# Four buffers of split weights in the expert stage, and products with the low part issued behind both column halves

## The chip, the core and the metric

The kernel runs on one core of one Trainium2 chip. The metric is the device time of one execution in microseconds (us), the median of several runs. An engine is named as the profile names it: PE is TensorE's matmul, PEld its weight load, DVE VectorE, ACT ScalarE, POOL GpSimd, SP SyncE, which issues most of the DMAs.

## What is computed

One layer of a hybrid encoder on 1024 tokens of width 2048 in float32: attention over a window and long convolutions side by side, an output projection, and then a mixture of 16 experts in which each expert picks its 128 tokens. The change lies in the experts alone:

```python
gate, idx = lax.top_k(jnp.swapaxes(affinity, 1, 2), cap)          # 16 experts, 128 tokens each
xg = jax.vmap(lambda hb, ib: hb[ib])(h, idx)
a = jnp.einsum('becd,edf->becf', xg, w_gate)                      # 2048 -> 1024
up = jnp.einsum('becd,edf->becf', xg, w_up)                       # 2048 -> 1024
ye = jnp.einsum('becf,efd->becd', jax.nn.silu(a) * up, w_down)    # 1024 -> 2048
ye = ye * gate[..., None].astype(ye.dtype)
# ... and each row of ye is added to the row of its token
```

## The kernel before

To keep float32 accuracy with the faster reduced float type, each operand is split in two: a high part, the value rounded by a copy on ACT (line 60), and a low part, what is left, by a subtraction on DVE (line 61). A product is then three matmuls (`mm3`, line 70): high token by high weight, high token by low weight, low token by high weight. In the expert stage (`phase3`) the tokens are the stationary operand and the weights stream, 512 columns at a time.

The raw weights of an expert come as 24 tiles of 1 MB: eight of the gate and eight of the up matrix in turn, then eight of the down matrix. They lie in a ring of 19 buffers (`EW`), taken in order by `load_expert`; two of the first expert's tiles lie in `el0` and `el1`, which later hold the expert's intermediate result `y` and its transposed, split form `h3`. SP issues a load as soon as its buffer has been let go. A raw tile is two half tiles of 128 x 1024; each is split into a pair `wh3`, `wl3`, of which there are three, so a new split has to wait until the matmuls of the third half tile before it have ended.

`gate_up` runs six steps of gate and up, half tile after half tile, six matmuls each (two column halves `n` of 512, three products). The last four raw tiles, the tail, are kept and gone through by column half: first all four half tiles for `n` = 0, then for `n` = 1, each step with the gate's 512 columns and the up's beside one another in one pair of split buffers. So the first column half of the result is ready early: `act(0)` makes SiLU(gate) x up of it (ACT line 1130, DVE line 1131), and `turn(0)` transposes it on TensorE in the third step of `n` = 1. `down` does the same with the down matrix, `turn(1)` behind its second raw tile, and the transposes of the next expert's tokens (`xh`, `xl`, from the gather of line 1090) behind the fourth to the seventh. Then ACT copies four banks with the gate's factor into `y` (line 1176) and POOL adds its rows to the output. Six PSUM banks are taken in turn by the two functions.

The order on TensorE is the program's, by `manual_schedule`. The orders on ACT, DVE and SP are laid down at compile time by the framework, which may put an instruction ahead of another that stands before it in the program; on the chip each of these engines then goes through its queue strictly in that order.

Of the kernel before, what the change touches and what calls it, by code (L numbers as in the profile page):

```python
# [8 lines left out]
R = mybir.dt.float32r  # L9
# [8 lines left out]
P = 128  # L18
D = 2048
S = 1024  # L20
KD = D // P
# [4 lines left out]
FF = 1024  # L26
# [11 lines left out]
class Block:  # L38
# [885 lines left out]
                            self.lane.append((t, c, first[t], xs[t]))  # L924
                        yield

    EW, EA = 19, 3
    EX = 2
    NW = KD + FF // P

# [138 lines left out]
    def phase3(self, ctx):  # L1069
        tc, nc, a = self.tc, self.nc, self.a  # L1070
        self.topk()
        pa = ctx.enter_context(tc.tile_pool(name="pa", bufs=1, space=PSUM, reuse_waits="tile"))
        pt_ = ctx.enter_context(tc.tile_pool(name="pt3", bufs=2, space=PSUM, reuse_waits="tile"))

        ex = ctx.enter_context(tc.tile_pool(name="ex", bufs=1, reuse_waits="tile"))
        self.ring(ctx, "ewb", 2, side="right")
        self.ring(ctx, "ewc", 8)
        el = self.el = ctx.enter_context(tc.tile_pool(name="el", bufs=1, reuse_waits="tile"))
        self.ring(ctx, "ewd", 6)
        xh = ex.tile([P, KD, P], R, name="xh", bufs=1)  # L1080
        xl = ex.tile([P, KD, P], R, name="xl", bufs=1)

        def bank():
            return pa.tile([P, 512], F32, name="pa", bufs=6)

        def gather(e):
            if e == NE:
                return
            xg = ex.tile([P, D + 16], F32, name="xg", bufs=1)
            nc.gpsimd.indirect_dma_start(out=xg, out_offset=None, in_=self.xg[:, :],  # L1090
                                         in_offset=bass.IndirectOffsetOnAxis(ap=self.idx[:, e:e + 1], axis=0))
            return xg

        def load():
            ahead = self.EW + max(min(self.used, KD - self.EX) + self.EX, self.used)
            while self.loaded < min(ahead, NE * self.NW):
                self.load_expert()

        def raw():
            load()  # L1100
            self.used += 1
            return self.eraw.pop(0)

        def parts():
            return (el.tile([P, FF], R, name="wh3", bufs=3), el.tile([P, FF], R, name="wl3", bufs=3))

        def half(w, i):
            wh, wl = parts()
            self.split(wh, wl, w[:, i * FF:i * FF + FF])
            return wh, wl  # L1110

        def gate_up(e):


            xg = self.xg3
            rs = ex.tile([P, 16], F32, name="rs", bufs=1)
            nc.scalar.copy(rs[:, 0:1], xg[:, D:D + 1])
            ps = {}
            for n in range(2):
                for j in range(2):  # L1120
                    ps[j, n] = bank()
            y = el.tile([P, 2 * FF], F32, name="el0", bufs=1)
            h3 = el.tile([P, 2, FF // P, P], R, name="el1", bufs=1)

            def product(j, n, k, wh, wl):
                self.mm3(ps[j, n], xh[:, k], xl[:, k], wh, wl, k == 0, k == KD - 1)

            def act(n):
                s = y[:, n * 512:n * 512 + 512]
                nc.scalar.activation(s, ps[0, n], AF.Silu, scale=rs[:, 0:1])  # L1130
                nc.vector.scalar_tensor_tensor(s, ps[1, n], rs[:, 0:1], s, op0=ALU.mult, op1=ALU.mult)

            def turn(n):
                self.turned(pt_, h3[:, 0], h3[:, 1], y, n)

            for kk in range(KD // 2 - 2):
                if kk == 2:
                    self.xg3 = gather(e + 1)
                for j in range(2):
                    w = raw() if kk or e else None  # L1140
                    for i in range(2):
                        wh, wl = half(w, i) if w is not None else ready.pop(0)
                        for n in range(2):
                            sl = slice(n * 512, n * 512 + 512)
                            product(j, n, 2 * kk + i, wh[:, sl], wl[:, sl])

            w = [raw() for j in range(4)]
            for n in range(2):
                for i in range(4):
                    wh, wl = parts()  # L1150
                    for j in range(2):
                        sl = slice(j * 512, j * 512 + 512)
                        c = i % 2 * FF + n * 512
                        self.split(wh[:, sl], wl[:, sl], w[i // 2 * 2 + j][:, c:c + 512])
                        if n == j == 1 and i == 2:
                            turn(0)
                        product(j, n, KD - 4 + i, wh[:, sl], wl[:, sl])
                act(n)
            return h3, y, lambda: turn(1)

        def down(e, h):
            h3, y, rest = h
            ps = [bank() for n in range(4)]
            for k in range(FF // P):
                w = raw()
                for c in range(2):
                    wh, wl = half(w, c)
                    for n in range(2):
                        sl = slice(n * 512, n * 512 + 512)
                        self.mm3(ps[2 * c + n], h3[:, 0, k], h3[:, 1, k], wh[:, sl], wl[:, sl], k == 0, k == FF // P - 1)  # L1170
                if k == 1:
                    rest()
                elif 3 <= k < 7 and self.xg3 is not None:
                    self.turned(pt_, xh, xl, self.xg3, k - 3, 2)
            for n in range(4):
                nc.scalar.activation(y[:, n * 512:n * 512 + 512], ps[n], AF.Copy, scale=self.gate[:, e:e + 1])  # L1176
            nc.gpsimd.indirect_dma_start(out=a["out"],
                                         out_offset=bass.IndirectOffsetOnAxis(ap=self.idx[:, e:e + 1], axis=0),
                                         in_=y, in_offset=None, compute_op=ALU.add)

        self.xg3 = gather(0)
        ready = []
        for j in range(2):
            w = raw()
            ready += [half(w, i) for i in range(2 - j)]
        ready.append(None)
        with tc.manual_schedule(engines={mybir.EngineType.PE}):
            for kg in range(4):
                self.turned(pt_, xh, xl, self.xg3, kg, 2)
            ready[3] = half(w, 1)  # L1190
            for e in range(NE):
                down(e, gate_up(e))
# [96 lines left out]
```

## Time and profile before

| | us |
|---|---|
| median of 3 runs (3375.63 to 3378.23) | 3376.8 |
| the profiled execution | 3381.3 |
| its span, first to last instruction | 3379.5 |
| TensorE busy in it | 3239.7 (96%) |
| VectorE busy | 2342.4 (69%) |
| ScalarE busy | 1848.0 (55%) |

The expert stage begins at about 2206 us, when the choice of tokens is done, and takes the rest of the span, about a third. TensorE's busy time counts a matmul from its start to its modelled end, and successive ones overlap; how densely they follow is read from their starts. The granted clock of TensorE is given as a share of full speed.

### The profile page before, as it was taken

The page shows a single profiled execution, that of the slowest core. Times are in us where ns is not written, and L with a number is a line of the kernel's source. Part 1 is how long each engine was busy: PE and PEld are TensorE (multiplying, and loading weights), DVE is VectorE, ACT ScalarE, POOL GpSimd, SP SyncE. Part 2 cuts the span into 40 slices and gives each one's busy share as a digit, 9 for nine tenths or more (in the row PEclk, how much of TensorE's full clock was granted, in tenths as well). Part 3 has the DMA queues.
Part 4 walks back from the last instruction along what each step waited for, and adds up shares of the span by engine and source line. Part 5 has one row for each costly group of instructions (what it writes and reads, how often), then busy time and mean ns, then how long its engine had stood idle before and what let it go on. Part 6 is the DMA issues. An engine that isn't in the chain of part 4 may idle for free.

```text
span 3379.5 us, 47125 instructions
## 1 busy us (share of the span) xinstructions
PE 3239.7 (96%) x17232; PEld 2794.5 (83%) x17232; DVE 2342.4 (69%) x3626; ACT 1848.0 (55%) x2956; POOL 87.9 (3%) x200
## 2 busy tenths in 40 slices
PE   8999999999999999999999999579999999999998
PEld 7899999987888888889977878467888877777776
DVE  5677766664666767667653333578889988888887
ACT  5455655443333433334453332258888877777776
POOL 0000000000000000000000000000000000000000
PEclk9999999999999999999999999789999999999999
DMA  7654555456566565555567554569999999999993
GB/s 244 198 166 163 167 173 194 159 157 221 181 197 194 191 196 184 194 193 167 168 213 240 188 200 138 217 262 376 377 393 387 389 382 370 375 384 365 384 379 107
DMA packets 286568, 830.67 MB, mean 246 GB/s; under 512 B 26341, under 2 KB 105360, under 8 KB 229761
## 3 DMA queue, kind: packets, MB, share of 16 engines
q1 hardware_dynamic: 280544, 791.12, 64.4%
q0 software_dynamic: 5648, 36.49, 4.1%
q8 instruction: 135, 2.21, 0.3%
q14 instruction: 97, 0.79, 0.1%
q10 hardware_dynamic: 144, 0.07, 0.0%
HBM read 751.71 MB, written 75.60 MB: 245 GB/s over the span
## 4 chain that ended last, share of the span: by engine, by line
PE 83%; DMA 6%; DVE 4%; ACT 4%; issue 2%; SPq 0%; POOLq 0%; POOL 0%; ACTq 0%; DVEq 0%
PE pj L68 29%; PE pa L68 27%; PE o L68 7%; PE c L68 5%; PE f L68 4%; PE a L68 3%; PE ct L79 2%; ACT wh L60 2%; DVE wl L61 2%; DMA w<-in_w_out_dram 2%; PE tp L1200 1%; PE a L79 1%; PE ft L79 1%; ACT el L1176 1%; DMA hl<-lo_d 1%
## 5 line engine op out<-in xcount | busy, mean ns | idle before, releaser
L60 ACT CAST wh<-w 128x1024 fp32r<-128x1024 f32 (+3 forms) x1368 | 1072.3, 795 | 778.8 <-PE pj L68 383.5
L61 DVE TENSOR_TENSOR wl<-w,wh 128x1024 fp32r<-128x1024 f32 (+3 forms) x1368 | 1219.6, 905 | 361.7 <-ACT wh L60 340.6
L68 PE MATMUL pa<-wl,xh 128*128 128x512 f32 x1024 | 409.0, 399 | 14.0 <-DVE wl L61 14.0
L68 PE MATMUL pa<-wh,xh 128*128 128x512 f32 x1024 | 407.8, 398 | 9.4 <-ACT wh L60 9.4
L68 PE MATMUL pa<-wh,xl 128*128 128x512 f32 x1024 | 404.8, 395 | 0.0
L68 PE MATMUL pa<-wh,el 128*128 128x512 f32 x1024 | 340.6, 399 | 0.0
L68 PE MATMUL o<-wh,m 128*128 128x512 f32 x1008 | 332.1, 403 | 0.7 <-ACT wh L60 0.7
L68 PE MATMUL pj<-wh,hh 128*128 128x384 f32 x896 | 315.9, 353 | 2.9 <-ACT wh L60 2.9
L68 PE MATMUL pj<-hh,wh 128*128 128x512 f32 x768 | 314.7, 410 | 0.0
L68 PE MATMUL pj<-hl,wh 128*128 128x512 f32 x768 | 304.8, 397 | 6.4 <-DMA hl<-lo_d 6.4
L68 PE MATMUL pj<-wl,hh 128*128 128x384 f32 x896 | 305.1, 341 | 0.0
L68 PE MATMUL pj<-wh,hl 128*128 128x384 f32 x896 | 304.3, 340 | 0.0
L68 PE MATMUL pj<-hh,wl 128*128 128x512 f32 x768 | 302.9, 395 | 0.0
L68 PEld LDWEIGHTS pa<-wl,xh 128*128 128x128 f32 x1024 | 193.5, 189 | 70.6 <-DVE wl L61 27.1
L68 PEld LDWEIGHTS pa<-wh,xh 128*128 128x128 f32 x1024 | 193.3, 189 | 58.5 <-ACT wh L60 13.4
L68 PEld LDWEIGHTS pa<-wh,xl 128*128 128x128 f32 x1024 | 193.4, 189 | 43.5
L68 PEld LDWEIGHTS pa<-wh,el 128*128 128x128 f32 x1024 | 193.1, 189 | 39.5
L68 PEld LDWEIGHTS o<-wh,m 128*128 128x128 f32 x1008 | 191.0, 191 | 39.0 <-ACT wh L60 1.8
L68 PE MATMUL pa<-wl,el 128*128 128x512 f32 x512 | 201.3, 393 | 0.0
L68 PE MATMUL o<-wl,m 128*128 128x512 f32 x504 | 198.9, 395 | 0.3 <-DVE wl L61 0.3
L68 PEld LDWEIGHTS pj<-wh,hh 128*128 128x128 f32 x896 | 169.7, 189 | 8.8 <-ACT wh L60 3.2
L68 PEld LDWEIGHTS pj<-hh,wl 128*128 128x128 f32 x768 | 144.5, 188 | 34.7
(304 smaller groups left out, 5301.5 us busy)
## 6 DMA issues: line engine op xcount, KB each, us to landing
hl<-lo_d SPq DMA_DIRECT2D x608, 256.0 KB, 3.0
w<-in_w_down_dram SPq DMA_DIRECT2D x128, 1024.0 KB, 11.2
w<-in_w_up_dram SPq DMA_DIRECT2D x127, 1024.0 KB, 8.1
w<-in_w_gate_dram SPq DMA_DIRECT2D x127, 1024.0 KB, 9.6
w<-in_w_at_dram SPq DMA_DIRECT2D x120, 384.0 KB, 3.5
w<-in_w_out_dram SPq DMA_DIRECT2D x64, 512.0 KB, 3.9
w<-in_w_hy_dram SPq DMA_DIRECT2D x96, 256.0 KB, 3.4
Hd<-H SPq DMA_DIRECT2D x32, 513.0 KB, 4.2
```

The lines of the kernel that those rows point to most:

```text
L60: nc.scalar.copy(hi, src)
L61: nc.vector.tensor_tensor(lo, src, hi.bitcast(F32), op=ALU.subtract)
L68: self.nc.tensor.matmul(out, w, x, start=start, stop=stop)
L79: self.nc.tensor.transpose(pt[:, i * P:(i + 1) * P], b, self.ident)
L1176: nc.scalar.activation(y[:, n * 512:n * 512 + 512], ps[n], AF.Copy, scale=self.gate[:, e:e + 1])
L1200: self.nc.tensor.transpose(pt[:, i * P:(i + 1) * P], src[:, c:c + (P - 1) * step + 1:step], self.ident)
```

## The change

The pairs of split weights become four. To make room, the ring of raw tiles loses one buffer (`EW` 18, and 5 instead of 6 in its last part); `xh` and `xl` move from the pool `ex`, which lies ahead of the ring's third part, into the pool `el` behind it, where the split weights are. `mm3` gives way in the expert stage to `products`, which takes two output banks: for each of them high by high and low token by high weight, and behind these four matmuls the two with the low weight. In the tail it pairs gate and up, and `turn(0)` stands ahead of the six matmuls of the third step, where it stood between its gate and its up products.

```diff
-    EW, EA = 19, 3
+    EW, EA = 18, 3
...
-        self.ring(ctx, "ewd", 6)
-        xh = ex.tile([P, KD, P], R, name="xh", bufs=1)
-        xl = ex.tile([P, KD, P], R, name="xl", bufs=1)
+        self.ring(ctx, "ewd", 5)
+        xh = el.tile([P, KD, P], R, name="xh", bufs=1)
+        xl = el.tile([P, KD, P], R, name="xl", bufs=1)
...
-            return (el.tile([P, FF], R, name="wh3", bufs=3), el.tile([P, FF], R, name="wl3", bufs=3))
+            return (el.tile([P, FF], R, name="wh3", bufs=4), el.tile([P, FF], R, name="wl3", bufs=4))
+
+        def products(out, hi, lo, wh, wl, start, stop):
+
+            parts_ = [(o, slice(i * 512, i * 512 + 512)) for i, o in enumerate(out)]
+            for o, sl in parts_:
+                self.mm(o, hi, wh[:, sl], start, False)
+                self.mm(o, lo, wh[:, sl], False, False)
+            for o, sl in parts_:
+                self.mm(o, hi, wl[:, sl], False, stop)
...
-            def product(j, n, k, wh, wl):
-                self.mm3(ps[j, n], xh[:, k], xl[:, k], wh, wl, k == 0, k == KD - 1)
...
-                        for n in range(2):
-                            sl = slice(n * 512, n * 512 + 512)
-                            product(j, n, 2 * kk + i, wh[:, sl], wl[:, sl])
+                        k = 2 * kk + i
+                        products([ps[j, 0], ps[j, 1]], xh[:, k], xl[:, k], wh, wl, k == 0, False)
...
-                        if n == j == 1 and i == 2:
-                            turn(0)
-                        product(j, n, KD - 4 + i, wh[:, sl], wl[:, sl])
+                    if n == 1 and i == 2:
+                        turn(0)
+                    k = KD - 4 + i
+                    products([ps[0, n], ps[1, n]], xh[:, k], xl[:, k], wh, wl, False, i == 3)
...
-                    for n in range(2):
-                        sl = slice(n * 512, n * 512 + 512)
-                        self.mm3(ps[2 * c + n], h3[:, 0, k], h3[:, 1, k], wh[:, sl], wl[:, sl], k == 0, k == FF // P - 1)
+                    products(ps[2 * c:2 * c + 2], h3[:, 0, k], h3[:, 1, k], wh, wl, k == 0, k == FF // P - 1)
```

## Rows read from the trace of the kernel before

**Rows 1.** The page, engines: busy us, share of the span, instructions.

```profile
PE 3239.7 (96%) x17232; PEld 2794.5 (83%) x17232; DVE 2342.4 (69%) x3626; ACT 1848.0 (55%) x2956; POOL 87.9 (3%) x200
```

**Rows 2.** Busy time by stretches: stretch, its us, PE, PEld, DVE, ACT, POOL, clock, DMA share, GB/s.

```profile
2300.00:2700.00 400.00, 396.56 (x1766) 320.83 (x1765) 360.53 (x365) 323.52 (x392) 18.65 (x10) 1.00 0.99 386
2800.00:3300.00 500.00, 485.00 (x2150) 388.73 (x2148) 437.64 (x442) 393.80 (x477) 23.31 (x13) 1.00 0.96 377
```

**Rows 3.** Waits from 2222 to 3370 us: us in total, times, longest.

```profile
PE pa L68 <- DVE wl L61: 14.0, 24, 0.7
...
PE pa L68 <- ACT wh L60: 9.4, 9, 1.1
```

**Rows 4.** SP's waits; software queue (packets, MB); loads (us to landing); from 2200 us.

```profile
SPq L953 <- DVE wl L61: 975.9, 361, 36.0
...
q0 software_dynamic: 4608, 33.69, 11.0%
...
w<-in_w_gate_dram SPq DMA_DIRECT2D x120, 1024.0 KB, 9.6
```

**Rows 5.** Chain of waits, early and late experts: start us, us, what, how many.

```profile
2406.56 0.44 PE tp L1200 x4
...
2491.76 2.78 PE pa L68 x12
2494.55 0.46 PE tp L1200 x4
...
2548.05 0.44 PE tp L1200 x4
...
2834.69 0.43 PE tp L1200 x4
...
2907.32 0.44 PE tp L1200 x4
```

**Rows 6.** Timeline at an expert's start, ACT and PE: start us, us, what.

```profile
2859.95 1.85 ACT L1176 ACTIVATE el<-pa,gate 128x512 f32<-128x512 f32 x3
...
2864.05 0.50 PE L68 MATMUL pa<-wl,xh 128*128 128x512 f32 x1 [0.69 <-DVE wl L61]
```

**Rows 7.** Timeline in the tail, ACT of an early expert, ACT and PE of a late one.

```profile
2396.14 1.14 ACT L60 CAST wh<-w 128x512 fp32r<-128x512 f32 x2 [0.24 <-PE pa L68]
...
2826.47 2.18 ACT L60 CAST wh<-w 128x512 fp32r<-128x512 f32 x4 [0.77 <-PE pa L68]
...
2828.18 0.49 PE L68 MATMUL pa<-wh,xh 128*128 128x512 f32 x1 [1.04 <-ACT wh L60]
```

**Rows 8.** Groups, 2300 to 3300 us, forms apart: count, busy us, mean ns, idle before.

```profile
L61 DVE TENSOR_TENSOR wl<-w,wh 128x1024 fp32r<-128x1024 f32 x556 | 678.0, 1225 | 92.7 <-ACT wh L60 83.2 <-DMA w<-in_w_gate_dram 1.0 <-DMA w<-in_w_down_dram 0.2
L60 ACT CAST wh<-w 128x1024 fp32r<-128x1024 f32 x557 | 585.1, 1054 | 162.8 <-PE pa L68 159.4 <-DMA w<-in_w_up_dram 1.3 <-DMA w<-in_w_down_dram 0.7
...
L60 ACT CAST xh<-tp 128x512 fp32r<-128x512 f32 x56 | 32.4, 578 | 0.0
```

**Rows 9.** Timeline at `turn(0)`, DVE and PE of an early expert, PE of the first.

```profile
2403.58 0.74 DVE L1131 SCALAR_TENSOR_TENSOR el<-pa,rs,el 128x512 f32<-128x512 f32 x1
...
2406.40 0.60 PE L1200 MATMUL tp<-ident,el 128*128 128x128 f32 x4
...
2263.66 0.63 PE L1200 MATMUL tp<-ident,el 128*128 128x128 f32 x4 [2.01 <-DVE el L1131]
...
2264.50 0.63 PE L68 MATMUL pa<-wl,xh 128*128 128x512 f32 x1
2264.93 0.63 PE L68 MATMUL pa<-wh,xl 128*128 128x512 f32 x1
```

**Rows 10.** Before the first expert: the last early loads, the first gather, a gather's landing.

```profile
2180.93 3.85 SPq L953 DMA_DIRECT2D w<-in_w_down_dram  x2
...
2208.26 1.03 POOL L1090 DMA_INDIRECT xg<-xg,idx  x1 [419.84 <-DVE idx L1066]
...
DMA to landing us min/median/max: 5.6/8.7/10.7
```

## The prediction

> **What bounds the kernel now.** I read the page first, then the engines' busy time by stretches, then the waits, then the chain of waits expert by expert, and last single instructions at the places that the chain names. The page says that TensorE is 96% busy [rows 1]; that share hides what matters here, since a matmul is shown longer than its share of the pipeline. The stretches are the better view: between 2300 and 2700 us the four hundred microseconds hold 396.6 us of TensorE, between 2800 and 3300 only 485.0 of 500 [rows 2]. So something that costs 2% begins on the way. The waits say what it is: in the whole expert stage TensorE waited 24 times for a low part (DVE, `wl`) and 9 times for a high part (ACT, `wh`) [rows 3], and for no load worth counting. SP's queue shows why not: its loads wait 361 times for a ring buffer that DVE has to let go [rows 4], so the ring of raw weights is full and TensorE, not the memory, sets the pace.
>
> The chain gives the size. From the transposes behind one expert's tail to those of the next it is (2548.05 - 2406.56)/2 = 70.7 us in the early experts and 2907.32 - 2834.69 = 72.6 us in the later ones [rows 5]. Undisturbed, twelve matmuls (one raw tile) take 2.78 us, 0.232 each, and four transposes 0.46 [rows 5]. An expert has 24 raw tiles and six groups of transposes: 24 x 2.78 + 6 x 0.46 = 69.5 us. So an early expert loses 1.2 us and a late one 3.1 us. There are two places.
>
> At the **start of an expert** ACT copies four finished outputs out of PSUM, three of them in one run of 1.85 us, and only then splits the next weights; TensorE stands until the low part behind it is there [rows 6]. This happens at 15 expert starts. In the **tail** (the last four half tiles of gate and up) the late experts have another order of copies on ACT: where an early expert shows pairs, each behind one buffer, a late one shows four copies in a row behind a wait for a buffer, and TensorE waits for a high part [rows 7] and then for a low one. 9 such waits for `wh` and 24 - 15 = 9 for `wl` say that it is nine experts. The order on ACT and DVE is laid down when the program is compiled (only TensorE's is written out by hand), and the trace does not say why it differs; copies in the order in which raw tiles were expected to arrive would give it: both gate halves, then both up halves, and a half of the second column side ahead of the up half that TensorE needs.
>
> **The change, part by part.** All of it against the profiled execution: span 3379.5, its own time 3381.3 us; the median of the three runs shown is 4.5 us less, and I take that off at the end.
>
> *Fourth buffer and later low products.* A half tile (six matmuls) is 1.39 us. Now a buffer comes free at the end of a half; the copy takes 1.05 and the subtraction 1.23 [rows 8], so 2.3 us later the low part is there, and it is wanted 2 x 1.39 + 0.23 = 3.0 us after the release: 0.7 us to spare, less than the output copies take. Then: `wh` is last read by the fourth matmul, so it is free 0.46 us before the end of its half; the split ends at 1.85 us; it is wanted three halves and four matmuls on, at 4.2 + 0.9 = 5.1 us. That leaves 3.2 us. The longest interruption on ACT is one token copy (0.58 [rows 8]) and four output copies (1.85/3 = 0.62 each [rows 6]), together 3.1 us. It fits, barely. DVE is the next engine: 360.5 us in 400 [rows 2], so 63.7 of the 70.7 us of an expert, below 69.5, and it has the halves between to catch up. I give the start 0.95 of the 1.2 us back: 15 x 0.95 = 14.3 us; bounds 0 (if the copies behind the outputs stay where they are) and 1.2.
>
> *Tail.* If the order stayed regular or harmless, the 72.6 - 70.7 = 1.9 us go in nine experts. If the order keeps following expected arrivals, a fourth buffer lets ACT run still further into the second column side: both of its first two halves (four copies, (2.18 - 0.62)/3 = 0.52 apart [rows 7]) can stand ahead of the up half that TensorE needs. That copy then ends about 1.2 us after the third half's turn began, and is wanted 0.46 into it: some 0.8 us lost; with both raw tiles late, by the same counting, 1.5. Bounds 0 and 1.9, I take 0.8, the middle of the three orders: 9 x (1.9 - 0.8) = 9.9 us. As the ring is a tile shorter, one more expert may fall into that order: -0.8.
>
> *Order of products.* Count, operands and output banks of the matmuls stay; twelve of them that change the bank every third time take 2.78 us [rows 5] without a gap, so changing costs 0 here. The gate sum now ends with the fifth matmul and not the third, so SiLU may start 0.46 us later.
>
> *Transposes of the first half of y.* They move ahead of three matmuls, 0.7 us earlier: four transposes on TensorE, one copy on ACT, one subtraction on DVE; no DMA, and neither SP nor POOL is passed. What waits for them is the third half of the tail, on TensorE. The product they read ends at 2403.58 + 0.74 = 2404.32, the transposes start at 2406.40 [rows 9]: 2.1 us of cover, less 0.7 and 0.46, leaves 0.9. Cost 0. In the first expert there is no cover: `y` lies in a buffer of raw weights that is read to the end of the tail, and TensorE waits 2.0 us, after which matmuls stand 0.43 apart for a while [rows 9]. Four buffers bring that release forward by about 1.9 us, the move takes 0.7 away: I count +1 us gained, bounds -0.7 and +4.
>
> *A ring tile less, token tiles moved.* No instruction is added; SBUF addresses shift, so the first loads may wait for another tile of the stage before. The last of those 20 loads is issued before 2185 us, the first gather, on which the stage hangs, at 2208.26 [rows 10]: over 20 us of cover, cost 0. Without it the gather would land later, by at most the spread of landings, 10.7 - 5.6 = 5.1 us [rows 10]. In steady state a tile is worth 70.7/24 = 2.9 us of the lead, and the earlier splits give 1.9 of it back.
>
> Sum: 14.3 + 9.9 - 0.8 + 1.0 = 24.4 us; 3381.3 - 24.4 = 3356.9, less 4.5 gives **3352 us**.
>
> **The loads as a bound.** A late expert moves 25.2 MB of weights and, from the software queue's total [rows 4], 33.7/16 = 2.1 MB of tokens and results, 27.3 MB; at 69.5 us that asks for 393 GB/s. The trace shows 386 over 400 us at a share of 0.99 [rows 2]. At 386 an expert would need 70.7 us, 1.2 more than TensorE, 18 us over 15 experts, which the lead (18 tiles of 2.9 us, less 9.6 for a landing [rows 4]: 43 us) covers. The Trainium skill, page "DMA: Bandwidth & Descriptors", sections Specifications and "Where 436 GB/s comes from", puts the limit of HBM for one core at about 358 GB/s and says that this side binds for loads into SBUF; by it an expert would take 27.3/0.358 = 76 us and this change could bring nothing. The 386 of the trace speaks against that figure here. By rows, the loads decide below about 377 GB/s: there they need 72.4 us, and 15 x 2.9 = 43 us is all of it.
>
> **Rivals.** (a) *All stalls go*, the order is harmless too: 14.3 + 9 x 1.9 + 1 = 32.4, so 3344. For it: only two places stall. Against: the compiled order differed in nine experts already. (b) *The order keeps the tail*: the 1.9 us stay and two more experts get them: 14.3 + 1 - 3.8 = 11.5, so 3365. (c) *Nothing moves*: the split behind the output copies stays behind them, and the tail stays as it is: 3376. (d) *Slower, by the transposes*: more copies ahead of SiLU in ACT's queue make the multiplication late, TensorE waits at the moved transposes in each expert as it does in the first (2.0 us, and some nine slow matmuls at 0.43 - 0.23 = 0.2 each, 3.8 in all [rows 9]): 15 x 3.8 - 24 = +33, so 3410. It costs something once SiLU starts more than 0.9 us later, and outweighs the gain at 0.9 + 24.4/15 = 2.5, that is behind five more copies of 0.52. For it: the first expert. Against: 2.1 us of cover now. (e) *Loads decide*: were the memory good for 5% less than the 386, 367 GB/s, an expert would need 74.4 us, and 15 x 4.9 - 43 = 30 us would be lost, more than the gain; half of that gives 3367. Against: SP waits for buffers, not for data.
>
> **How the numbers follow.** Forecast 0.46, (a) 0.20, (b) 0.16, (c) 0.08, (d) 0.06, (e) 0.04. The forecast's own spread is 0 to 1.5 us in nine tails, about 3344 to 3360; (a) with the whole 1.2 us at the starts reaches 3340, (b) with a little less at the starts 3368. From 3339 to 3368 leaves out (c), (d), (e) and some edges, under 0.2. A change within 0.2% (6.8 us) is about what a measurement of this kernel cannot tell from none. Faster than that are the forecast, (a), (b) and some of (e): 0.84; the same (c) and the rest of (e): 0.10; slower (d): 0.06.
>
> **What would show it.** The waits of TensorE for `wl` should fall from 24 to near none: that is the start. The period should be near 69.7 us in early experts, and where ACT's tail keeps its irregular order, near 70.5 and not 72.6, with one wait for `wh` and none for `wl`. SP should still wait for DVE. I am wrong at the start if the split behind the output copies still ends late; at the tail if four copies still stand behind a buffer wait and TensorE loses over 1.5 us; and altogether if a wait for the multiplication appears at the moved transposes beyond the first expert.

## The result and the profile after

The changed kernel takes 3331.8 us (median of 4 runs, 3326.74 to 3332.62) against 3376.2 of the kernel before on the same chip: ratio 0.9868, 95% interval 0.9851 to 0.9885. It is 44 us faster; forecast were 24, and the time lies 7 us below the lower end of the range. The profiled execution has a span of 3330.3 us, 49.2 less than before.

Engines of the page, after (busy us, share of the span, instructions), for [rows 1]:

```profile
PE 3205.7 (96%) x17232; PEld 2790.5 (84%) x17232; DVE 2332.9 (70%) x3626; ACT 1842.3 (55%) x2956; POOL 77.7 (2%) x200
```

Busy time by stretches, after, with the columns of [rows 2]:

```profile
2300.00:2700.00 400.00, 399.16 (x1823) 331.01 (x1822) 367.12 (x376) 332.73 (x407) 18.34 (x12) 1.00 1.01 400
2800.00:3300.00 500.00, 494.09 (x2238) 406.09 (x2239) 452.58 (x463) 408.60 (x497) 20.02 (x13) 1.00 0.95 370
```

Waits of TensorE and of SP in the expert stage, after (us in total, times, longest), for [rows 3, 4]:

```profile
PE pa L68 <- ACT wh L60: 8.4, 10, 0.8
PE tp L1204 <- DVE el L1137: 0.9, 1, 0.9
...
SPq L953 <- DVE wl L61: 933.3, 362, 35.1
```

The number of instructions is the same, and so is the share of 96%. What changed is seen in the stretches: in the same 400 us of an undisturbed part TensorE now does 1823 matmuls and transposes, where it did 1766, at the same granted clock of 1.00. The waits for a low part, 24 before, are gone. The waits for a high part are still there, ten instead of nine and each shorter (longest 0.8 instead of 1.1). SP still waits for DVE to let a ring buffer go, and not for data.

Chain of waits, after (start us, us, what, how many): from one `turn(0)` to the next in an early expert, and the same in a late one, for [rows 5]:

```profile
2391.09 0.44 PE tp L1204 x4
...
2415.40 0.47 PE tp L1204 x4
2415.87 43.58 PE pa L68 x192
2459.45 0.44 PE tp L1204 x4
...
2944.80 0.44 PE tp L1204 x4
...
2969.59 37.69 PE pa L68 x166
3007.28 0.02 issue
3007.31 1.67 ACT wh L60 x3
3008.97 0.04 issue
3009.02 5.51 PE pa L68 x22
3014.53 0.44 PE tp L1204 x4
```

An early period is 2459.45 - 2391.09 = 68.4 us (70.7 before), a late one 3014.53 - 2944.80 = 69.7 (72.6 before). In an early expert the chain now runs over TensorE alone. And there is the surprise: from the last transposes of the tokens to `turn(0)` 192 matmuls, 12 of `down` and 180 of `gate_up`, follow each other in 43.58 us, 227 ns each. I had taken 2.78/12 = 232 ns as the floor. The chain of the kernel before had a row right beside the one that I took, in the same expert, that did not fit this floor, 24 matmuls of `down` in 5.47 us, 228 ns each:

```profile
2485.82 5.47 PE pa L68 x24
```

Late experts keep one stop. Timeline of TensorE and ACT, after (start us, us, what, [idle before <- releaser]), in the tail of a late expert, for [rows 7]:

```profile
2728.89 0.39 PE L68 MATMUL pa<-wh,xl 128*128 128x512 f32 x1
2730.13 0.50 PE L68 MATMUL pa<-wh,xh 128*128 128x512 f32 x1 [0.84 <-ACT wh L60]
...
2728.41 2.18 ACT L60 CAST wh<-w 128x512 fp32r<-128x512 f32 x4 [0.22 <-PE pa L68]
```

Four copies still stand in a row on ACT, and TensorE needs the third of them: the matmul starts 1.24 us behind its neighbour instead of 0.23. With what follows it, a late expert is 69.73 - 68.37 = 1.36 us longer than an early one.

So by the profiles: from the first `turn(0)` to the last, sixteen of them, it was 1079.5 us and is 1039.1, 40.5 less. From the first gather to the first `turn(0)` it was 2263.66 - 2208.26 = 55.4 us [rows 9, 10] and is 52.1, 3.3 less:

```profile
2202.10 1.02 POOL L1090 DMA_INDIRECT xg<-xg,idx  x1 [422.96 <-DVE idx L1066]
...
2254.18 0.63 PE L1204 MATMUL tp<-ident,el 128*128 128x128 f32 x4 [0.94 <-DVE el L1137]
```

Another 6.2 us lie before the first gather, where nothing was changed, and the end behind the last `turn(0)` is 0.7 us longer. Twelve kernels of this study that differ only in the expert stage issue that gather between 2196.4 and 2208.3 us, so these 6 us are the spread of profiled executions. What there is to explain are 43 to 44 us.

### The profile page after: what moved, and what is told of

Read it like the earlier page. It is cut to its first block, busy times and chain, and to the rows that moved or that the text cites. A ratio compares the mean times of both kernels' runs of the same rounds, so it can differ in the third digit from the quotient of the medians.

```text
span 3330.3 us, 47541 instructions
## 1 busy us (share of the span) xinstructions
PE 3205.7 (96%) x17232; PEld 2790.5 (84%) x17232; DVE 2332.9 (70%) x3626; ACT 1842.3 (55%) x2956; POOL 77.7 (2%) x200
## 4 chain that ended last, share of the span: by engine, by line
PE 87%; DMA 5%; DVE 3%; issue 2%; ACT 2%; SPq 0%; POOLq 0%; POOL 0%; ACTq 0%; DVEq 0%
PE pj L68 30%; PE pa L68 29%; PE o L68 8%; PE c L68 6%; PE f L68 4%; PE a L68 3%; PE ct L79 2%; DMA w<-in_w_out_dram 2%; PE tp L1204 1%; ACT wh L60 1%; PE a L79 1%; PE ft L79 1%; DMA x<-in_x_dram 1%; PE l L68 1%; DMA hl<-lo_d 1%
## 5 line engine op out<-in xcount | busy, mean ns | idle before, releaser
L68 PE MATMUL pa<-wl,xh 128*128 128x512 f32 x1024 | 318.0, 391 | 0.0
L68 PE MATMUL pa<-wh,el 128*128 128x512 f32 x1024 | 283.9, 399 | 0.0
L68 PEld LDWEIGHTS pj<-wl,hh 128*128 128x128 f32 x896 | 169.8, 190 | 3.0 <-DVE raw L732 1.6
```

Of the source, the lines that this page charges most:

```text
L68: self.nc.tensor.matmul(out, w, x, start=start, stop=stop)
```

## The experiments

The theories at the outset: T1, four buffers and the low products behind the high ones take the stalls away, as forecast; T2, beside that the matmuls themselves follow more closely, and this comes from one of three things, the place of `xh` and `xl`, the order of the products with its change of banks, or the fourth buffer. The parts of the change were taken apart first, in four kernels on one chip (before there 3369.5). Ratios are to the kernel before on the same chip; the two periods given are those of early and of late experts.

**Tokens back to their old pool**, the rest as changed.

```diff
-        xh = el.tile([P, KD, P], R, name="xh", bufs=1)
-        xl = el.tile([P, KD, P], R, name="xl", bufs=1)
+        xh = ex.tile([P, KD, P], R, name="xh", bufs=1)
+        xl = ex.tile([P, KD, P], R, name="xl", bufs=1)
```

> The changed kernel with the split token tiles xh and xl back in their old pool, ahead of the ring; the orders on PE, DVE, ACT and POOL are those of the changed kernel. After the change a matmul of gate and up follows the last one after 227 ns where it was 232 before, worth some 16 us in the stage, which the prediction did not have. Theory 'place': the 5 ns come from where the stationary tokens lie; then the matmuls are at 232 again and the time is 15 to 18 us above the changed kernel, about 3348. Theory 'lead': they come from the splits being ready well ahead; then 227 stays and the time is that of the changed kernel within 3 us, about 3332.

Measured: 3347.8 us, ratio 0.9936 (0.9919 to 0.9952). Periods 69.4 and 70.7. The order of instructions on TensorE, ACT, DVE and POOL is the changed kernel's, and so are the waits of TensorE (10 for `wh`, 8.1 us; none for `wl`); only the pace of the matmuls is the old one. Chain of waits, tokens back:

```profile
2418.96 44.61 PE pa L68 x192
```

The same 192 matmuls take 44.61 us, 1.03 more. So the place of two tiles, on which no instruction and no wait hangs, is worth 1.0 us in each expert, 1054.4 - 1039.1 = 15.3 us from the first `turn(0)` to the last.

**Tokens moved alone**, all else as before.

```diff
-        xh = ex.tile([P, KD, P], R, name="xh", bufs=1)
-        xl = ex.tile([P, KD, P], R, name="xl", bufs=1)
+        xh = el.tile([P, KD, P], R, name="xh", bufs=1)
+        xl = el.tile([P, KD, P], R, name="xl", bufs=1)
```

> The kernel before with only xh and xl moved beside the split weights; ring of 19, three split buffers, old order of products. Theory 'place': gate and up matmuls at 227 ns, some 15 us faster than before, about 3361. Theory 'lead': 232 ns as before, no change, 3376 within 4 us. Both: the waits at expert starts and in the tails stay (24 for the low part, 9 for the high part).

Measured: 3355.1 us, ratio 0.9961 (0.9946 to 0.9976), periods 69.7 and 71.8, 1.0 and 0.9 below before. The waits stay. Waits of TensorE, tokens moved alone:

```profile
PE pa L68 <- DVE wl L61: 14.8, 24, 0.8
PE pa L68 <- ACT wh L60: 9.6, 9, 1.1
```

**The order of products alone** (and the earlier `turn(0)` with it): the changed kernel with three pairs of buffers, the ring of 19 and the tokens in their old pool.

```diff
-    EW, EA = 18, 3
+    EW, EA = 19, 3
...
-        self.ring(ctx, "ewd", 5)
-        xh = el.tile([P, KD, P], R, name="xh", bufs=1)
-        xl = el.tile([P, KD, P], R, name="xl", bufs=1)
+        self.ring(ctx, "ewd", 6)
+        xh = ex.tile([P, KD, P], R, name="xh", bufs=1)
+        xl = ex.tile([P, KD, P], R, name="xl", bufs=1)
...
-            return (el.tile([P, FF], R, name="wh3", bufs=4), el.tile([P, FF], R, name="wl3", bufs=4))
+            return (el.tile([P, FF], R, name="wh3", bufs=3), el.tile([P, FF], R, name="wl3", bufs=3))
```

> The kernel before with only the order of products and the earlier transposes; ring of 19, three split buffers, tokens in the old place. The low part is wanted 0.7 us later and the high part's buffer is free 0.46 us earlier, so the margin for a split grows from 0.7 to 1.9 us: the start stall (about 1.1 us in 15 experts) should shrink to some 0.3, 12 us. Theory 'place': matmuls stay at 232 ns, about 3360. Theory 'lead': with twice the margin most matmuls come at 227, another 10 to 15 us, about 3347. The tails stay as before or lose a little less.

Measured: 3353.3 us, ratio 0.9953 (0.9938 to 0.9967), periods 69.8 and 71.1; 232.6 ns from start to start. Waits of TensorE, order alone:

```profile
PE pa L68 <- ACT wh L60: 7.3, 9, 0.8
PE tp L1204 <- DVE el L1137: 2.2, 1, 2.2
```

**The fourth buffer alone** (and a ring of 18), products in the old order, tokens in the old pool.

```diff
-    EW, EA = 19, 3
+    EW, EA = 18, 3
...
-        self.ring(ctx, "ewd", 6)
+        self.ring(ctx, "ewd", 5)
...
-            return (el.tile([P, FF], R, name="wh3", bufs=3), el.tile([P, FF], R, name="wl3", bufs=3))
+            return (el.tile([P, FF], R, name="wh3", bufs=4), el.tile([P, FF], R, name="wl3", bufs=4))
```

> The kernel before with only the fourth split buffer (and the ring of 18 that pays for it); old order of products, tokens in the old place. The margin for a split grows from 0.7 to 2.1 us: the start stall shrinks to 0.1 to 0.3 us, some 13 us. Theory 'place': matmuls stay at 232 ns; with the tails as in the changed kernel (1.4 us each in ten experts) about 3360. Theory 'lead': 227 ns, about 3345.

Measured: 3359.0 us, ratio 0.9965 (0.9951 to 0.9979), periods 69.4 and 71.4, 232.6 ns. Waits of TensorE, fourth buffer alone:

```profile
PE pa L68 <- ACT wh L60: 10.5, 10, 1.1
PE pa L68 <- DVE wl L61: 3.9, 10, 0.4
```

What follows from the four: each of the two parts clears most of the start of an expert by itself (early periods 69.4 with the buffer, 69.8 with the order, 69.4 with both, 70.7 with neither), so there they stand in for one another. In the tail the fourth buffer does nothing (a late expert is 71.43 - 69.45 = 1.98 us longer than an early one, as before) and makes it one expert more; the order of products alone shortens it, to 1.3 us. That fits with the low part of a late split being wanted later: with the old order matmuls wait for it ten times (3.9 us), with the new one none does. The new pace comes with the place alone; bank order and buffer number do not touch it.

**Why does the place matter?** The compiled programs list the address of each tile in a partition. In both kernels `wh3` and `wl3` begin 448 bytes past a multiple of 512, that is 192 past a multiple of 256. The tokens began at 320 (64 past a multiple of 256) and after the move begin at 448. Theory 'phase': a matmul whose stationary and streamed tile have the same offset starts every 227 ns, with different offsets every 233. Rival 'neighbourhood': what counts is in which pool, near what, the tokens lie. Both predict the runs so far; they part where the offset is moved and the pool is not. Four more kernels on the same chip, measured beside one another (before there 3367.3).

**Tokens in the old pool, 128 bytes further**, so that they have the offset of the weights:

```diff
-        xh = el.tile([P, KD, P], R, name="xh", bufs=1)
-        xl = el.tile([P, KD, P], R, name="xl", bufs=1)
+        xh = ex.tile([P, KD * P + 32], R, name="xh", bufs=1)[:, 32:].rearrange("p (k t) -> p k t", k=KD)
+        xl = ex.tile([P, KD * P + 96], R, name="xl", bufs=1)[:, :KD * P].rearrange("p (k t) -> p k t", k=KD)
```

> The changed kernel with xh and xl back in their old pool as in the first experiment, but 128 bytes further on in each partition (everything behind them moves by 512). The first experiment showed matmuls of gate and up at 232 to 233 ns there, against 227 beside the split weights. Its tokens lay at 320 bytes past a multiple of 512 and the split weights at 448; beside them both lie at 448, and here again both lie at 448. Theory 'region': what counts is how far down in the memory the tokens lie; 232.6 ns stay, time as in the first experiment, 16 us above the changed kernel. Theory 'phase': what counts is the tokens' and the weights' offset within a row of 512 bytes; 226.7 ns, time of the changed kernel within 3 us.

Measured: 3335.2 us, ratio 0.9892 (0.9872 to 0.9912), periods 68.4 and 69.7. Chain, old pool shifted:

```profile
2422.00 43.58 PE pa L68 x192
```

**Tokens beside the weights, 384 bytes further**, so that they have their old offset again:

```diff
-        xh = el.tile([P, KD, P], R, name="xh", bufs=1)
-        xl = el.tile([P, KD, P], R, name="xl", bufs=1)
+        xh = el.tile([P, KD * P + 96], R, name="xh", bufs=1)[:, 96:].rearrange("p (k t) -> p k t", k=KD)
+        xl = el.tile([P, KD * P + 32], R, name="xl", bufs=1)[:, :KD * P].rearrange("p (k t) -> p k t", k=KD)
```

> The changed kernel, xh and xl beside the split weights, but 384 bytes further on, so that they lie at 320 bytes past a multiple of 512 and the split weights at 448, as in the kernel before (everything behind them moves by 512; all orders are those of the changed kernel). Theory 'region': 226.7 ns, time of the changed kernel. Theory 'phase': 232.6 ns, 16 us above the changed kernel.

Measured: 3345.8 us, ratio 0.9938 (0.9913 to 0.9962), periods 69.4 and 70.7; the changed kernel itself, beside it, 3333.9. Chain, beside and shifted:

```profile
2416.11 44.61 PE pa L68 x192
```

Both fall as 'phase' has it, and 'neighbourhood' is out: the old pool is as fast as the new one with the right offset, the new one as slow as the old with the wrong one.

These runs leave one more rival, that the tokens' own offset counts (192 past a multiple of 256 fast, 64 slow) and not its match with the weights, which lie at 192 in the expert stage of every kernel here. The output projection speaks against it. By the compiled programs its stationary tile `m` and its streamed `wh` and `wl` all begin 64 past a multiple of 256, in the kernel before too. Timeline of TensorE in it, before, two matmuls that stand 24 apart:

```profile
1859.87 0.39 PE L68 MATMUL o<-wl,m 128*128 128x512 f32 x1
...
1865.31 0.39 PE L68 MATMUL o<-wl,m 128*128 128x512 f32 x1
```

That is 5.44 us for 24 steps, 227 ns each, where the same kernel's tokens, at 64 too but against weights at 192, give 233. So a stationary tile at 64 is not slow by itself.

**The tail's copies in program order.** The changed kernel, in which ACT is held to the program's order for the copies of the last four half tiles, by a framework call that orders an instruction behind another on its engine:

```diff
-        nc.scalar.copy(hi, src)
-        nc.vector.tensor_tensor(lo, src, hi.bitcast(F32), op=ALU.subtract)
+        c = nc.scalar.copy(hi, src); nc.vector.tensor_tensor(lo, src, hi.bitcast(F32), op=ALU.subtract)
+        return c.ins
...
+            last = None
...
-                        self.split(wh[:, sl], wl[:, sl], w[i // 2 * 2 + j][:, c:c + 512])
+                        with ExitStack() as behind:
+                            if last is not None:
+                                behind.enter_context(tc.issue_after(last))
+                            last = self.split(wh[:, sl], wl[:, sl], w[i // 2 * 2 + j][:, c:c + 512])
```

> The changed kernel with the order of ACT's copies in the tail fixed to the order in which TensorE wants them (gate and up in turn). In the changed kernel ten experts wait once for a high part in the tail and take 69.7 us where the others take 68.4. Theory: that is the order of the copies alone; then all experts take 68.4, the ten waits go, 10 x 1.36 = 13.6 us less than the changed kernel. Rival: the raw tiles do come late there, or DVE is the limit; then the wait only moves and nothing is gained.

Measured: 3322.0 us, ratio 0.9866 (0.9847 to 0.9885); the changed kernel beside it 3333.9. All fifteen periods are 68.4 us, and the stage from first to last `turn(0)` is 1025.6 us, 13.5 less, about 10 x 1.36. Timeline of ACT in the tail of a late expert, then waits of TensorE in the stage (all there are), then busy time by stretches, tail in order:

```profile
2722.04 1.14 ACT L60 CAST wh<-w 128x512 fp32r<-128x512 f32 x2 [0.30 <-PE pa L68]
2723.40 1.14 ACT L60 CAST wh<-w 128x512 fp32r<-128x512 f32 x2 [0.22 <-PE pa L68]
2724.76 1.14 ACT L60 CAST wh<-w 128x512 fp32r<-128x512 f32 x2 [0.22 <-PE pa L68]
```

```profile
PE tp L1208 <- DVE el L1137: 0.9, 1, 0.9
```

```profile
2300.00:2700.00 400.00, 400.00 (x1828) 332.05 (x1828) 367.04 (x377) 333.37 (x407) 18.50 (x12) 1.00 1.01 401
2800.00:3300.00 500.00, 500.00 (x2283) 414.38 (x2282) 452.56 (x470) 413.39 (x506) 20.93 (x13) 1.00 0.93 369
```

Pairs of copies, each behind one buffer, in place of four in a row: what was left of the tail was the order laid down at compile time. Holding ACT's copies changes more than ACT, though: the compiled program differs from the changed kernel's in 188 places of ACT's order and in 274 of DVE's (and in none of the other engines'), so ACT's share by itself is not shown. TensorE is busy for the whole of both stretches.

**The changed kernel once more**, as the measure for the three before it.

> The changed kernel itself, beside the three others: some 40 us below the kernel before, gate and up matmuls at 226.7 ns.

Measured: 3333.9 us, ratio 0.9899 (0.9882 to 0.9915), periods 68.4 and 69.7.

Two questions were left: does the rule hold for other tiles, and over what period do offsets count? Four kernels on another chip (before there 3371.1).

**The input projection aligned.** There the weights `wh`, `wl` and the tokens' low part `hl` begin 128 bytes past a multiple of 512 and the tokens' high part `hh` at 320, so 128 against 64 past a multiple of 256. The 512-column products stream the tokens past the weights, the 384-column ones the weights past the tokens.

```diff
-        self.mh = hc.tile([P, 5, 2, 258], R, name="mh")
+        self.mh = hc.tile([P, 80 + 5 * 2 * 258], R, name="mh")[:, 80:].rearrange("p (a b c) -> p a b c", a=5, b=2)
```

> The changed kernel with one thing outside the expert stage: 320 bytes of padding at one end of the pool behind the input projection's weights, so that its streamed tiles (wh, wl, hl), which begin 128 bytes past a multiple of 512, begin 320 past one, as its token tiles hh do. The compiled order of every engine stays. Theory 'phase is general': the 512-column matmuls of the projection, now 231 to 236 ns apart, come to about 227, the 384-column ones from 175 to 180 to about 171; some 2,000 of the first and 2,400 of the second: 2,000 x 7 + 2,400 x 5 = 26 us of TensorE, all of it saved if TensorE bounds that stage: 3333.8 - 26 = 3308, 15 to 25 us less than the changed kernel being likely. Rival 'held by others' (the stage waits for ACT, DVE and loads between the matmuls): pitches fall, the time stays within 5 us of the changed kernel's. Rival 'only the experts': pitches stay where they are.

Measured: 3324.6 us (3319.67 to 3329.95), ratio 0.9863 (0.9827 to 0.9899). The first gather, a mark for the end of all that comes before the experts, is issued at 2190.7 us, 6 us ahead of the earliest of the twelve kernels with the old offsets:

```profile
2190.74 1.03 POOL L1090 DMA_INDIRECT xg<-xg,idx  x1 [414.38 <-DVE idx L1066]
```

The steps from start to start of the 512-column products fell from 231 to 234 ns to 229 to 231, the middle one of the three 384-column products from 176.9 to 175.4, and the two others not. That is 3 ns on two thousand matmuls and 1.5 on nine hundred, 8 us, a third of what 'phase is general' asked; there the matmuls are mixed with those of attention and convolution, and many stand behind something else. And one of the products does not fit the rule as it was put: `hl` by `wh` had the same offset, 128, before the padding too, and yet its step to the next matmul was 233 ns and fell to 229 when the tiles around it were aligned as well. The two tiles of a matmul alone do not settle its step there. By the medians 6 us separate this kernel from the one with 256 bytes below, whose pace is the changed kernel's and which ran on the same chip, and the intervals overlap. The direction is as the theory has it, the size is not, and whether the rule is the whole story in that stage stays open.

**Both, the aligned projection and the tail in order.**

> The padding of the run before together with the tail's copies in program order (e7_tail_in_order). The two act in different stages, so the gains should add: 12 us below the run before, about 3297 by 'phase is general', about 3320 by the two rivals.

Measured: 3314.9 us (3302.66 to 3318.3), ratio 0.9832 (0.9797 to 0.9867), the lowest of all; 10 us below the run before, where the tail by itself gave 12, and between the two sums expected. Its first gather is issued at 2185.4 us. Its interval still touches that of the tail alone.

**Tokens 256 bytes further**, and **64 bytes further**, beside the weights (the second with 16 and 112 in place of 64 and 64):

```diff
-        xh = el.tile([P, KD, P], R, name="xh", bufs=1)
-        xl = el.tile([P, KD, P], R, name="xl", bufs=1)
+        xh = el.tile([P, KD * P + 64], R, name="xh", bufs=1)[:, 64:].rearrange("p (k t) -> p k t", k=KD)
+        xl = el.tile([P, KD * P + 64], R, name="xl", bufs=1)[:, :KD * P].rearrange("p (k t) -> p k t", k=KD)
```

> The changed kernel with the token tiles of the expert stage 256 bytes further, so that they begin 192 bytes past a multiple of 512 where the split weights begin 448 past one. Order of every engine as changed. If what counts is the offset within 256 bytes, this is aligned: pitch 226.7 ns, periods 68.4 and 69.7, as the changed kernel (3334). If it is the offset within 512 bytes: pitch 232.6, periods 69.4 and 70.7, 12 to 16 us more.

> The changed kernel with the token tiles 64 bytes further (0 past a multiple of 512, against 448 of the split weights). If any mismatch within the period costs the same: pitch 232.6, periods 69.4 and 70.7, 12 to 16 us more than the changed kernel. If the cost grows with the distance, or only blocks of 128 bytes or more count: pitch 226.7 to 230 and a time in between or equal.

Measured: 3330.5 us, ratio 0.988 (0.9844 to 0.9916), with 256 bytes; 3352.3 us, ratio 0.9941 (0.9923 to 0.9959), with 64. Chain of waits, 256 bytes further:

```profile
2410.82 43.56 PE pa L68 x192
```

Chain of waits, 64 bytes further:

```profile
2423.93 44.78 PE pa L68 x192
```

256 bytes apart is as good as no distance, 227 ns; 64 bytes apart costs a little more than 128, 233.3 ns against 232.6, and the early periods are 69.6 us against 69.4. In this stage the offset that counts is the one within 256 bytes, and the two mismatches tried cost 6 to 7 ns a matmul.

## Why the prediction was wrong

**Bound and place of the stalls: right.** TensorE set the pace, and it stood at the starts and in the tails only. With both stops gone (the tail in order) it is busy 400.00 of 400.

**The start of an expert: right, a little too small.** Said were 0.95 of 1.2 us in 15 experts, 14.3 us; measured with the old offset (tokens back) are 70.67 - 69.40 = 1.27 us, and no matmul waits for `wl`. That is 19 us. The count of buffers was right, but it was not the only way there: the order of products gives 0.9 of the 1.27 us without the fourth buffer. The prediction counted both in one term and did not ask what the order gives alone.

**The tail: the mechanism was right, the size was not.** ACT's order stayed irregular, got one expert more, as said, and four copies still stand in a row. The residue is 1.3 us and not 0.8, against 2.0 before: 9 x 0.66 - 1.3 = 4.6 us, where 9.9 - 0.8 = 9.1 were said. At the wait itself TensorE loses 1.24 - 0.23 = 1.0 us, near the 0.8 said; I had counted nothing for the matmuls behind it, whose low parts come late as well (two weight loads on, `PEld` waits 0.37 us for `wl`).

**The first expert**: the wait for `y` fell from 2.0 to 0.9 us (0.8 with the old offset), which gave 2.5 us up to the first `turn(0)`. The slow matmuls behind it are gone as well: that is the 1.4 us by which the first period, 72.1 us before, was longer than the next (tokens back, 69.5 against 69.4). Together 3.9 us; said was +1, bounds -0.7 and +4. The prediction read the slow matmuls, 0.43 us apart, off the timeline and did not ask why they were slow; the granted clock shows it. Busy time by stretches, before and then after, with the columns of [rows 2]:

```profile
2222.00:2262.00 40.00, 39.65 (x171) 31.82 (x169) 35.62 (x37) 31.44 (x37) 0.00 (x0) 1.00 0.88 335
2262.00:2270.00 8.00, 6.34 (x23) 5.18 (x24) 5.59 (x6) 5.67 (x8) 0.00 (x0) 0.79 0.47 163
```

```profile
2254.18:2258.00 3.82, 3.82 (x19) 3.26 (x20) 3.79 (x4) 3.36 (x4) 0.00 (x0) 1.00 0.44 154
```

Before, TensorE had stood for 2.0 us and the clock fell from 2.4 to 1.2 GHz for some of the next matmuls (0.79 is the mean of the stretch); after, it stood for 0.9 us and the clock stayed at 1.00.

Together, with the tokens in their old place, these terms come to 1079.5 - 1054.4 = 25.1 us between the `turn(0)`s and 2.5 ahead of them, 27.6 against 24.4 forecast; the medians of that kernel and of the one before are 22 us apart. That the sums agree so well is partly luck: the start was put 5 us too low and the tail 4.5 us too high.

**Token tiles moved: this is the step that failed.** It was put at 0, because no instruction is added and the first loads have cover; the addresses were looked at for what they do to waits and not for what they do to the matmuls that read them. They were worth 15.3 us in the stage and 0.8 in its first part, 16 us, and this is what lies outside the range. A second step made the failure invisible: 'undisturbed, twelve matmuls take 2.78' was taken as the floor for all 24 raw tiles, so even rival (a), with all stalls gone, ended at 3344, at 3340 with the whole 1.2 us at the starts. In `down`, whose stationary tile `h3` always had the offset of the weights, 24 matmuls took 5.47 us in the trace of before. Two paces for one kind of matmul in one chain was the hint, and no allowance was made for another pace. (The 2.78 come from raw tiles right behind the tokens' transposes. Twelve matmuls there take 2.76 to 2.80 us in every kernel, the aligned ones too; the first ten or so steps behind the transposes average 230 to 232 ns, the later ones 227, and why is open.)

**Order of products, 0**: right for the pace, which did not change with the banks (order alone, 232.6 ns).

**The rivals.** (a) and (b) are each half of what happened: the starts went as in (a), two thirds of the tail stayed. (c) is out. (d) is out: TensorE waits for the multiplication once, in the first expert, 0.9 us, and the clock drop that its price rested on is gone even there. (e) is out as well: over 400 us the loads moved 400 GB/s, and in the kernel with the tail in order 401, while SP waited for buffers. The Trainium skill, page "HBM Reference", section Specifications (TRN2), says that a core which streams alone gets well above its share of the domain, about 425 GB/s; the rows agree with that, and not with the 358 GB/s that the prediction weighed. At 27.3 MB for an expert, 68.4 us ask for 399 GB/s, which is what was moved: how much further the loads would go is not shown by any run.

## What to carry to other kernels

Before a tile is called free to move, compare its offset within 256 bytes with that of the tile it meets in a matmul: here a mismatch cost 6 of 233 ns on nearly every one of 192 products in an expert, without a wait that any view shows. Then measure, for in the input projection aligning gave 1 to 4 ns on the 512-column products and next to nothing on the 384-column ones. Take the pace of TensorE from all rows that have it, per matmul and per kind; where like matmuls show two paces, the faster one is the floor. When a stall is an order laid down at compile time, forcing the order is worth more than another buffer: the buffer left 1.3 us in each of ten tails, the order none.

## What the hardware showed that was not expected

In the fourteen profiles the step from start to start of the gate and up matmuls, 128 x 128 by 512 columns of the reduced float type at a granted clock of 1.00, fell into two groups: 227 ns in all eight in which `xh`, `xl` and the split weights begin at the same offset modulo 256 bytes (apart by 0 or 256), and 232 to 233 ns in the six where they don't (apart by 64 or 128). Two pairs of runs show that it is the offset and not the pool: the old pool without and with 128 bytes of padding, 233 and 227; the new one without and with 384, 227 and 233. The weights' offset was not moved in this stage; that the match counts and not the tokens' offset alone rests on the output projection, where both lie at 64 and the step is 227 ns. What in the chip reads the two tiles so that this matters, no run here shows.
